# Turning and splitting queries and keys of two token tiles at a time, with the gate and pooling projections issued in even steps over the heads of a differential-attention encoder layer

## The chip, the cores and the metric

The kernel runs on one core of one Trainium2 chip. The metric is the device time of one execution in microseconds (us): lower is better. Three runs of the kernel before gave 1553.82, 1554.85 and 1556.53 us; their median is 1554.85 us.

## What is computed

One residual layer on 1024 tokens of 1024 channels, in float32. The part that the change touches is the projection of the normalised input h, and what attention makes of queries and keys:

```python
h = rmsnorm(x, g_mix[l])
z = h @ w_in[l]                                  # pooling channels | q | k | v
y_pool = pool_mixer(u_pool, w_pool_grp[l], pool_scale[l])
y_attn = diff_attention(q, k, v, ...)            # 8 heads, two softmax maps each, 64 channels a map
gates = sigmoid(h @ w_gate[l] + b_gate[l])
merged = gates[..., :D] * (y_pool @ w_branch_pool[l]) + gates[..., D:] * (y_attn @ w_branch_attn[l])
x = x + merged @ w_out[l]
x = x + square(relu(rmsnorm(x) @ w_up[l])) @ w_down[l]
```

The pooling mixer takes, for each of four groups of 128 channels, the mean over the last 2, 4, 8 or 16 tokens minus the token itself, and multiplies it by a 128x128 matrix.

## The kernel before

Every float32 operand of a matmul is split into a high part (rounded to the type that TensorE takes, by a cast on ScalarE) and a low part (the rest, by a subtraction on VectorE, or on GpSimd for weights). A product is then three matmuls into one PSUM bank: high x high, high x low, low x high. The helpers are `split` (L117 the cast, L118 the subtraction) and `mm3` (L123, L124, L125).

The work of the heads is a pipeline over 64 steps, one for each head h (8) and token tile t (8 tiles of 128 tokens). The loop over g at L645 runs one stage for each of several token tiles in every step, with the delays of the string `O`: A computes the projections z of a tile (24 matmuls of 384 columns), B normalises q and k and splits v (VectorE, ScalarE, GpSimd; the tile qn), C turns qn by transposes on TensorE into the bank tk and splits it into K and Q (`stage_qkT`, L453), D computes scores sc, their minimum (VectorE, L502) and the exponential (ScalarE, L510), E turns the attention weights s into the tiles AT (bank ta, L555, then split), F multiplies them by V (bank po), H and R the norm of the result (trr is a transpose of R), W loads and splits the next head's weights.

In stage C each map m of a tile takes three casts on ScalarE (L468, L470, L473) and three subtractions on VectorE (L469, L471, L472), on 64 partitions and 128 columns. The banks tk, ta and trr share two PSUM banks (`ps_t`).

Behind that loop in the code stand the gate and pooling projections, called units here: 16 column blocks of w_gate and four pooling groups, each for two halves of 512 tokens, so 40 units of 24 matmuls of 512 columns (g and u). A unit loads its weights by SP's queue (`fill_w`), splits them with ScalarE and GpSimd, multiplies, is emptied by ScalarE (`go`, L745, or L710 and L737) and stored by a DMA that ScalarE issues. A unit up to gate column 12, and all of the pooling group's, use the one bank of `ps_f`; the later columns alternate with the two banks of z. `pool_group` also makes running sums on VectorE (L719 to L728) and copies on GpSimd (L718).

The order of each engine is not the order of the code. A scheduler picks, for each engine, the next instruction among those that it holds to be ready, with the code's order as priority. The units at the end of the code are thus fetched forward into the heads. Behind the heads come the branch projections (bp, ba), the output projection (op), the feed-forward layer (X, Y, Z, W, then Da, Db).

Of the kernel before, what the change touches and what calls it, by code (L numbers as in the profile page):

```python
# [8 lines left out]
F32 = mybir.dt.float32  # L9
# [3 lines left out]
ALU = mybir.AluOpType  # L13
# [18 lines left out]

N_U, N_W, N_RAW, N_V = 11, 8, 2, 6
N_FW, N_FR, N_FO = 4, 2, 2
N_Q, N_QN = 3, 2
N_Z, N_S, N_T, N_F = 2, 2, 2, 1
N_YU = 5
N_QKVW = 8 * H
# [17 lines left out]
def encoder_kernel(  # L56
# [55 lines left out]
    def f(ap):  # L112
        return ap.bitcast(F32)
# [28 lines left out]
    def fr_tile(shape, name):  # L142
        return fp.tile(shape, F32, tag="fr", name=name, bufs=N_FR)
# [142 lines left out]
        }  # L286


    with ExitStack() as ph:
        sp = ph.enter_context(tc.tile_pool(name="sp", bufs=1))  # L290
        ps_s = ph.enter_context(tc.tile_pool(name="ps_s", bufs=N_S, space=PSUM))
# [161 lines left out]
        def stage_qkT(h, t):  # L453

            th, c0 = t // 4, (t % 4) * P
            K, qn = KV[h][0][th], st[h, t]["qn"]
            tr = ps_t.tile([P, 512], F32, tag="tr", name=f"tk{h}_{t}")
            for i in range(2):
                nc.tensor.transpose(
                    tr[:, i * P : (i + 1) * P], qn[:, 2 * i : 2 * i + 2, :].rearrange("p a b -> p (a b)"), identf  # L460
                )
            Q = sp.tile([P, 2, 2, P], F32R, tag="Q", name=f"Q{h}_{t}", bufs=N_Q)
            halves = (slice(0, HD), slice(HD, P))
            for m in range(2):
                own, other = halves[m], halves[1 - m]
                q, k = tr[own, 0:P], tr[own, P : 2 * P]
                k_hi, q_hi = K[own, m, c0 : c0 + P], Q[own, m, 0, :]
                nc.scalar.copy(k_hi, k)  # L468
                nc.vector.tensor_tensor(K[other, m, c0 : c0 + P], k, f(k_hi), op=ALU.subtract)  # L469
                nc.scalar.copy(q_hi, q)  # L470
                nc.vector.tensor_tensor(Q[other, m, 0, :], q, f(q_hi), op=ALU.subtract)  # L471
                nc.vector.tensor_tensor(Q[own, m, 1, :], q, f(q_hi), op=ALU.subtract)  # L472
                nc.scalar.copy(Q[other, m, 1, :], q)  # L473
            st[h, t]["Q"] = Q
            yield

        def stage_scores(h, t):
# [189 lines left out]
    def fill_w(src, c0, name):  # L667
        ws = []
        for j in range(2):
            rw = fr_tile([P, 4, P], f"fr{name}_{j}")  # L670
            nc.sync.dma_start(
                rw, src[j * 512 : (j + 1) * 512, c0 : c0 + P].rearrange("(kk p) c -> p kk c", p=P)
            )
            w = fw_tile([P, 2, 4, P], f"fw{name}_{j}")
            split(w[:, 0], w[:, 1], rw, nc.gpsimd)
            ws.append(w)
        return ws

    nb = [0]

    def spare_bank(name):

        nb[0] += 1
        pool, tag = (ps_f, "f") if nb[0] % 3 == 0 else (ps_z, "z")
        return pool.tile([P, 512], F32, tag=tag, name=name)

    def fill_bank(name):
        return ps_f.tile([P, 512], F32, tag="f", name=name)

    def fill_proj(ws, th, name, bank_fn=fill_bank):  # L690
        ps = bank_fn(name)
        for k in range(NK):
            w = ws[k // 4]
            mm3(
                ps, w[:, 0, k % 4, :], w[:, 1, k % 4, :],
                hT[k // 2, th, 0][:, k % 2, :], hT[k // 2, th, 1][:, k % 2, :], k == 0, k == NK - 1,
            )
        return ps

    def pool_group(g):  # L700
        win = WINDOWS[g]
        ws = fill_w(w_in, g * P, f"pool{g}")
        rg = fr_tile([P, P], f"rgrp{g}")
        nc.sync.dma_start(rg, w_pool_grp[g])
        wg = fq.tile([P, 2, P], F32R, tag="wg", name=f"wgrp{g}")
        split(wg[:, 0, :], wg[:, 1, :], rg, nc.gpsimd)
        u = fu_tile(f"u{g}")
        for th in range(2):
            ps = fill_proj(ws, th, f"u{g}_{th}")
            nc.scalar.copy(u[:, th * 512 : (th + 1) * 512], ps)  # L710

            n0 = 16 * th
            src = u[:, 512 * th - n0 : 512 * (th + 1)]
            n = 512 + n0
            cur, sh = src, 1
            while sh < win:
                nxt = fo_tile(f"sum{g}_{th}_{sh}")
                nc.gpsimd.tensor_copy(nxt[:, 0:sh], cur[:, 0:sh])  # L718
                nc.vector.tensor_tensor(nxt[:, sh:n], cur[:, sh:n], cur[:, 0 : n - sh], op=ALU.add)  # L719
                cur = nxt  # L720
                sh *= 2
            e = 0
            if th == 0:
                e = win - 1
                nc.vector.tensor_tensor(cur[:, 0:e], cur[:, 0:e], inv[:, 0:e], op=ALU.mult)
                nc.vector.tensor_tensor(cur[:, 0:e], cur[:, 0:e], src[:, 0:e], op=ALU.subtract)
            e += n0
            nc.vector.scalar_tensor_tensor(  # L728
                cur[:, e:n], cur[:, e:n], 1.0 / win, src[:, e:n], op0=ALU.mult, op1=ALU.subtract
            )  # L730
            m = fq.tile([P, 2, 512], F32R, tag="mx", name=f"mix{g}_{th}")
            split(m[:, 0, :], m[:, 1, :], cur[:, n0:n])
            yield
            ps = ps_f.tile([P, 512], F32, tag="f", name=f"yp{g}_{th}")
            mm3(ps, wg[:, 0, :], wg[:, 1, :], m[:, 0, :], m[:, 1, :], True, True)
            yp = fo_tile(f"yps{g}_{th}")
            nc.scalar.activation(yp[:, 0:512], ps, AF.Copy, scale=cols[:, 16 + g : 17 + g])  # L737
            nc.scalar.dma_start(p_dram[g * P : (g + 1) * P, th * 512 : (th + 1) * 512], yp[:, 0:512])

    def gate_cols(c):  # L740
        ws = fill_w(w_gate, c * P, f"gate{c}")
        for th in range(2):
            ps = fill_proj(ws, th, f"g{c}_{th}", spare_bank if c >= G_Z else fill_bank)
            fo = fo_tile(f"go{c}_{th}")
            nc.scalar.activation(fo[:, 0:512], ps, AF.Identity, bias=cols[:, c : c + 1])  # L745
            nc.scalar.dma_start(g_dram[c * P : (c + 1) * P, th * 512 : (th + 1) * 512], fo[:, 0:512])
            yield

    def gates():
        for c in range(2 * NK - 2):  # L750
            yield from gate_cols(c)
        for gen in [gate_cols(c) for c in (2 * NK - 2, 2 * NK - 1)] * 2:
            next(gen)
            yield
# [569 lines left out]
```

## Time and profile before

| what | value |
|---|---|
| median of three runs | 1554.85 us (1553.82 to 1556.53) |
| span of the profiled execution, first to last instruction | 1551.6 us |
| median of the runs less that span | 3.2 us |
| granted TensorE clock | 1.000 |
| instructions in the span | 22088 |
| heads (z, attention and the units) | about 10 to 700 us |

The profile is of one execution. The span is the time from its first to its last instruction; the runs' time has a little around it. PE is TensorE's matmuls, PEld its weight loads, DVE is VectorE, ACT ScalarE, POOL GpSimd, SP the queue that issues most DMAs. Busy times are shares of the span; "idle before" is the idle time of an engine ahead of an instruction, with the instruction that ended it.

### The profile page before, as it was taken

To read this page: it belongs to the slowest core of one execution; us is meant where nothing else is said; L and a number is where in the kernel's file an instruction comes from. 1 tells how busy PE (TensorE), PEld (TensorE's weight loads), DVE (VectorE), ACT (ScalarE), POOL (GpSimd) and SP (SyncE) were. 2 spreads that over 40 slices of the span, in tenths; PEclk is the share of its full clock that TensorE was granted. 3 is DMA by queue.
4 is the path that set the end of the run, shared out by engine and by line. 5 is a ranking of instruction groups with operands and counts; after the bars stand their busy time and mean duration, and the time that the engine had idled before them with its cause. 6 is when DMAs were issued, how large, how long until landed. Compare 5 with 4: busy or idle time off the path is not lost.

```text
span 1551.6 us, 22088 instructions
## 1 busy us (share of the span) xinstructions
PE 1533.6 (99%) x7649; PEld 1320.8 (85%) x7649; DVE 1011.3 (65%) x2277; ACT 816.7 (53%) x1810; POOL 354.8 (23%) x449
## 2 busy tenths in 40 slices
PE   7999999999999999999999999999999999999999
PEld 6999999999998989888888887888888788888887
DVE  7777677777878787746422458866665667556662
ACT  6656556656566555645532547565555633333331
POOL 5433334243525262324363400000000000000000
PEclk9999999999999999999999999999999999999999
DMA  7111212021202031248536534554343799437650
GB/s 229 51 53 48 66 41 68 24 75 37 75 28 83 28 96 42 69 147 284 179 122 210 168 112 124 182 185 155 129 142 109 278 334 370 170 122 257 224 190 27
DMA packets 168009, 206.94 MB, mean 133 GB/s; under 512 B 10117, under 2 KB 104026, under 8 KB 167898
## 3 DMA queue, kind: packets, MB, share of 16 engines
q1 hardware_dynamic: 150490, 178.23, 35.0%
q10 hardware_dynamic: 17408, 27.30, 4.7%
q8 instruction: 60, 0.98, 0.3%
q14 instruction: 51, 0.42, 0.1%
HBM read 150.94 MB, written 54.56 MB: 132 GB/s over the span
## 4 chain that ended last, share of the span: by engine, by line
PE 89%; DVE 4%; DMA 3%; ACT 1%; issue 1%; POOL 1%; SPq 0%; ACTq 0%; POOLq 0%; DVEq 0%
PE z L125 5%; PE z L123 5%; PE z L124 5%; PE Da L124 4%; PE Da L123 4%; PE Da L125 4%; PE g L123 3%; PE g L124 3%; PE g L125 3%; PE Db L124 3%; PE Db L123 3%; PE Db L125 3%; PE X L125 2%; PE X L123 2%; PE X L124 2%; PE sc L499 2%
## 5 line engine op out<-in xcount | busy, mean ns | idle before, releaser
L123 PE MATMUL z<-wqkv,hT 128*128 128x384 f32 x512 | 174.7, 342 | 0.4 <-DVE qn L441 0.3
L125 PE MATMUL z<-wqkv,hT 128*128 128x384 f32 x512 | 174.3, 341 | 0.5 <-DVE hT L118 0.5
L124 PE MATMUL z<-wqkv,hT 128*128 128x384 f32 x512 | 173.8, 339 | 0.0
L510 ACT ACTIVATE s<-s,nm 128x256 f32<-128x256 f32 (+7 forms) x128 | 99.6, 778 | 49.2 <-DVE nm L502 44.1
L249 POOL TENSOR_TENSOR ms<-ms,mhalf 128x4 f32<-128x4 f32 x64 | 66.6, 1040 | 157.7 <-DVE ms L248 139.1
L125 PE MATMUL g<-hT,fwgate 128*128 128x512 f32 x256 | 101.0, 394 | 0.0
L124 PE MATMUL g<-hT,fwgate 128*128 128x512 f32 x256 | 100.9, 394 | 0.0
L123 PE MATMUL g<-hT,fwgate 128*128 128x512 f32 x256 | 100.9, 395 | 0.0
L123 PEld LDWEIGHTS z<-wqkv,hT 128*128 128x128 f32 x512 | 96.9, 189 | 4.2 <-DVE qn L441 1.0
L125 PEld LDWEIGHTS z<-wqkv,hT 128*128 128x128 f32 x512 | 96.7, 189 | 3.3 <-DVE hT L118 1.3
L124 PEld LDWEIGHTS z<-wqkv,hT 128*128 128x128 f32 x512 | 96.8, 189 | 2.9
L502 DVE CUSTOM_DVE_ANT_0 s<-sc,dist 128x512 f32<-128x512 f32 (+3 forms) x128 | 74.7, 586 | 22.1 <-PE sc L500 20.7
L118 POOL TENSOR_TENSOR wqkv<-rqkv,wqkv 128x384 fp32r<-128x384 f32 x60 | 63.3, 1072 | 17.7 <-ACT wqkv L117 15.3
L499 PE MATMUL sc<-K,Q 128*128 128x512 f32 (+2 forms) x192 | 67.2, 355 | 0.1
L118 DVE TENSOR_TENSOR AS<-s,AS 128x512 fp32r<-128x512 f32 x64 | 43.8, 687 | 35.8 <-ACT AS L117 35.6
L500 PE MATMUL sc<-K,Q 128*128 128x512 f32 (+2 forms) x192 | 66.6, 354 | 0.0
L473 ACT CAST Q<-tk 64x128 fp32r<-64x128 f32 x128 | 33.2, 260 | 58.6 <-DVE Q L472 56.8
L447 POOL TENSOR_TENSOR qn<-qn,ggh 128x128 f32<-128x128 f32 x64 | 32.6, 510 | 137.5 <-DVE qn L441 124.2
L470 ACT CAST Q<-tk 64x128 fp32r<-64x128 f32 x128 | 33.1, 259 | 50.5 <-DVE K L469 49.1
L118 POOL TENSOR_TENSOR fwgate<-frgate,fwgate 128x512 fp32r<-128x512 f32 x32 | 45.2, 1416 | 52.2 <-ACT fwgate L117 52.0
L125 PEld LDWEIGHTS g<-hT,fwgate 128*128 128x128 f32 x256 | 48.1, 188 | 8.6
L123 PEld LDWEIGHTS g<-hT,fwgate 128*128 128x128 f32 x256 | 48.2, 188 | 7.1
(429 smaller groups left out, 4649.6 us busy)
## 6 DMA issues: line engine op xcount, KB each, us to landing
wd<-in_w_down_dram SPq DMA_DIRECT2D x56, 512.0 KB, 5.5
wu<-in_w_up_dram SPq DMA_DIRECT2D x32, 512.0 KB, 5.3
udS<-us SPq DMA_DIRECT2D x64, 256.0 KB, 2.5
ur<-udS SPq DMA_DIRECT2D x32, 512.0 KB, 3.2
rqkv<-in_w_in_dram SPq DMA_DIRECT2D x64, 192.0 KB, 2.8
ud<-u ACTq DMA_DIRECT2D x48, 256.0 KB, 2.2
ur<-ud SPq DMA_DIRECT2D x24, 512.0 KB, 5.5
frgate<-in_w_gate_dram SPq DMA_DIRECT2D x32, 256.0 KB, 2.6
```

The costliest lines, as they stand in the source:

```text
L118: return (lo_eng or nc.vector).tensor_tensor(lo, src, f(hi), op=ALU.subtract)
L123: nc.tensor.matmul(ps, lhs_hi, rhs_hi, start=first, stop=False, **kw)
L124: nc.tensor.matmul(ps, lhs_hi, rhs_lo, start=False, stop=False, **kw)
L125: nc.tensor.matmul(ps, lhs_lo, rhs_hi, start=False, stop=last, **kw)
L249: nc.gpsimd.tensor_tensor(dst, dst, mhalf[:, :n], op=ALU.pow)
L447: nc.gpsimd.tensor_tensor(qn[:, 2:4, :], qn[:, 2:4, :], ggh.unsqueeze(1).broadcast_to([P, 2, HD]), op=ALU.mult)
L470: nc.scalar.copy(q_hi, q)
L473: nc.scalar.copy(Q[other, m, 1, :], q)
L499: nc.tensor.matmul(dst, Q[:, i, 0, :], rhs, start=True, stop=False)
L500: nc.tensor.matmul(dst, Q[:, i, 1, :], rhs, start=False, stop=True)
L502: nc.vector.tensor_tensor_reduce(out=s[i][:, c : c + w], in0=sc[:, 0:w], in1=dist[:, o0 + c : o0 + c + w], scale=2.0 ** -(h + 1), scalar=B ...
L510: nc.scalar.activation(s[i][:, 0:n], s[i][:, 0:n], AF.Exp, bias=last, scale=-1.0, accum_out=Z[:, i, t : t + 1])
```

## The change

Stage C runs once for two token tiles, at the odd one: four transposes fill the whole bank tk (queries of both tiles in the first half, keys in the second), and each of the twelve casts and subtractions covers 256 columns. Buffers: two tiles Q of twice the width instead of three, three qn instead of two. All stages behind C start one step later. The units' functions move ahead of the heads' loop, and the loop issues them itself: from step 5 on, half a unit for each step, 34 in all; six are left for the end. With that, their place in the code's order, and so their priority, is among the heads.

```diff
-N_Q, N_QN = 3, 2
+N_Q, N_QN = 2, 3
...
-O = "B1 C2 H6 D3 R7 E4 F5 W-2 A0"
+O = "B1 C2 H7 D4 R8 E5 F6 W-2 A0"
 ORDER = [(w[0], int(w[1:])) for w in O.split()]
 G_FIRST, G_Z = 13, 13
+F_FROM, F_PACE, F_UNITS = 4, 0.5, 34
...
+    def fillers():
+        gate_units = gates()
+        for _ in range(G_FIRST):
+            next(gate_units)
+            yield
+        for g in range(4):
+            for _ in pool_group(g):
+                yield
+                next(gate_units)
+                yield
+        for _ in gate_units:
+            yield
...
         def stage_qkT(h, t):
 
             th, c0 = t // 4, (t % 4) * P
-            K, qn = KV[h][0][th], st[h, t]["qn"]
+            K = KV[h][0][th]
             tr = ps_t.tile([P, 512], F32, tag="tr", name=f"tk{h}_{t}")
-            for i in range(2):
-                nc.tensor.transpose(
-                    tr[:, i * P : (i + 1) * P], qn[:, 2 * i : 2 * i + 2, :].rearrange("p a b -> p (a b)"), identf
-                )
-            Q = sp.tile([P, 2, 2, P], F32R, tag="Q", name=f"Q{h}_{t}", bufs=N_Q)
+            tk = tr.rearrange("p (s t q) -> p s t q", s=2, t=2)
+            for j in range(2):
+                qn = st[h, t + j]["qn"]
+                for i in range(2):
+                    nc.tensor.transpose(
+                        tk[:, i, j, :], qn[:, 2 * i : 2 * i + 2, :].rearrange("p a b -> p (a b)"), identf
+                    )
+            Q = sp.tile([P, 2, 2, 2 * P], F32R, tag="Q", name=f"Q{h}_{t}", bufs=N_Q)
             halves = (slice(0, HD), slice(HD, P))
+            c1 = c0 + 2 * P
             for m in range(2):
                 own, other = halves[m], halves[1 - m]
-                q, k = tr[own, 0:P], tr[own, P : 2 * P]
-                k_hi, q_hi = K[own, m, c0 : c0 + P], Q[own, m, 0, :]
+                q, k = tr[own, 0 : 2 * P], tr[own, 2 * P : 4 * P]
+                k_hi, q_hi = K[own, m, c0:c1], Q[own, m, 0, :]
                 nc.scalar.copy(k_hi, k)
-                nc.vector.tensor_tensor(K[other, m, c0 : c0 + P], k, f(k_hi), op=ALU.subtract)
+                nc.vector.tensor_tensor(K[other, m, c0:c1], k, f(k_hi), op=ALU.subtract)
                 nc.scalar.copy(q_hi, q)
                 nc.vector.tensor_tensor(Q[other, m, 0, :], q, f(q_hi), op=ALU.subtract)
                 nc.vector.tensor_tensor(Q[own, m, 1, :], q, f(q_hi), op=ALU.subtract)
                 nc.scalar.copy(Q[other, m, 1, :], q)
-            st[h, t]["Q"] = Q
+            for j in range(2):
+                st[h, t + j]["Q"] = Q[:, :, :, j * P : (j + 1) * P]
             yield
...
-            elif w == "C":
-                yield from stage_qkT(h, t)
+            elif w == "C" and t % 2:
+                yield from stage_qkT(h, t - 1)
...
-        for g in range(-2, N + 8):
+        units, made = fillers(), 0
+        for g in range(-2, N + 10):
...
+            while made < F_UNITS and made < (g - F_FROM) * F_PACE:
+                next(units)
+                made += 1
+        for _ in units:
+            pass
...
-    gate_units = gates()
-    for _ in range(G_FIRST):
-        next(gate_units)
-    for g in range(4):
-        for _ in pool_group(g):
-            next(gate_units)
-    for _ in gate_units:
-        pass
```

What the scheduler makes of it is shown at three places. Names are the program's, with head and tile behind the letter (AT0_3_4l is of head 0 and the fourth pair of tiles); "ISA" on VectorE is the fused add with minimum (L502) or the sum of squares (L593).

The first is on VectorE, at the end of head 0, ahead of the subtraction into AT0_3_4l that frees a transposed bank. Before:

```order
L517 RECIPROCAL cf0_7_1286<-Z0_361 128x1
L518 SCALAR_TENSOR_TENSOR cf0_7_1286<-cf0_7_1286,Z0_361,nlam_233 128x1
L437 TENSOR_REDUCE ms1_4_1532<-sq1_4_1531 128x4
L593 ISA oq0_2_1309,SS0_362<-po0_2_1261,identf_90 128x128
L593 ISA SS0_362 128x1
L519 SCALAR_TENSOR_TENSOR s0_7_0_1241<-s0_7_1_1242,cf0_7_1286,s0_7_0_1241 128x1024
L593 ISA oq0_2_1309,SS0_362<-po0_2_1261,identf_90 128x128
L593 ISA SS0_362 128x1
L248 TENSOR_SCALAR ms1_4_1532<-ms1_4_1532 128x4
L118 TENSOR_TENSOR AT0_3_4l_1251<-ta0_6_1_1290,AT0_3_4h_1250 128x3x128
```

After, at the same subtraction:

```order
L627 RECIPROCAL cf0_7_1372<-Z0_361 128x1
L628 SCALAR_TENSOR_TENSOR cf0_7_1372<-cf0_7_1372,Z0_361,nlam_233 128x1
L119 TENSOR_TENSOR AT0_3_4l_1337<-ta0_6_1_1376,AT0_3_4h_1336 128x3x128
L629 SCALAR_TENSOR_TENSOR s0_7_0_1327<-s0_7_1_1328,cf0_7_1372,s0_7_0_1327 128x1024
L703 ISA oq0_2_1395,SS0_362<-po0_2_1347,identf_90 128x128
```

The subtraction into AT0_3_4l stood behind the product over s0_7 of 1024 columns (L519) and two sums; now it stands ahead of them (L629 is that product).

The second is on VectorE, in head 6, at the first subtraction into AT6_1_0l and the running sums of pooling group 3 (sum3_0). Before:

```order
L719 TENSOR_TENSOR sum3_0_4_8118<-sum3_0_2_8115 128x508
L719 TENSOR_TENSOR sum3_0_8_8121<-sum3_0_4_8118 128x504
L728 SCALAR_TENSOR_TENSOR sum3_0_8_8121<-sum3_0_8_8121,u3_8085 128x497
L725 TENSOR_TENSOR sum3_0_8_8121<-sum3_0_8_8121,inv_99 128x15
L502 ISA s6_4_1_5977,nm6_4_5978<-sc6_4_1_0_5999,dist_229 128x512
L502 ISA nm6_4_5978 128x1
L726 TENSOR_TENSOR sum3_0_8_8121<-sum3_0_8_8121,u3_8085 128x15
L118 TENSOR_TENSOR AT6_1_0l_5851<-ta6_2_0_5854,AT6_1_0h_5850 128x3x128
L502 ISA s6_4_1_5977,nm6_4_5978<-sc6_4_1_512_6003,dist_229,nm6_4_5978 128x128
```

After:

```order
L612 ISA s6_4_0_6638,nm6_4_6640<-sc6_4_0_512_6664,dist_229,nm6_4_6640 128x128
L612 ISA nm6_4_6640 128x1
L119 TENSOR_TENSOR AT6_1_0l_6498<-ta6_2_0_6501,AT6_1_0h_6497 128x3x128
L546 TENSOR_TENSOR qn6_7_6631<-z6_7_6522,ms6_7_6624 128x256
L342 TENSOR_TENSOR sum3_0_1_6605<-u3_6578 128x511
L612 ISA s6_4_1_6639,nm6_4_6640<-sc6_4_1_0_6669,dist_229 128x512
L612 ISA nm6_4_6640 128x1
L119 TENSOR_TENSOR AT6_1_0l_6498<-ta6_3_0_6645,AT6_1_0h_6497 128x4x128
L342 TENSOR_TENSOR sum3_0_2_6608<-sum3_0_1_6605 128x510
L612 ISA s6_4_1_6639,nm6_4_6640<-sc6_4_1_512_6673,dist_229,nm6_4_6640 128x128
```

All the sums of group 3 now come behind the subtraction out of ta6_2_0 (the first, of 511 columns, right behind the next qn), and the long ones behind the subtraction out of ta6_3_0 as well.

The third is on TensorE near the end of the heads, between the units g11_0 and g11_1, that share the one bank of `ps_f`. Before:

```order
L125 MATMUL g11_0_8290<-hT3_0_0_147,fwgate11_1_8287 128x512
L499 MATMUL sc7_4_1_512_6806<-K7_1_6089,Q7_4_6656 128x256
L459 MATMUL tk7_5_6759<-identf_90,qn7_5_6650 128x128 x2
L500 MATMUL sc7_4_1_0_6802<-K7_0_6088,Q7_4_6656 128x512
L500 MATMUL sc7_4_1_512_6806<-K7_1_6089,Q7_4_6656 128x256
L555 MATMUL ta7_3_0_6786<-identf_90,s7_3_6669 128x128 x4
L123 MATMUL g11_1_8318<-hT0_1_0_321,fwgate11_0_8282 128x512
```

After (the transposes ta7_4_0 and two matmuls of po7_1 stand just ahead):

```order
L126 MATMUL g11_0_7657<-hT3_0_0_147,fwgate11_1_7654 128x512
L124 MATMUL g11_0_7657<-hT3_0_0_147,fwgate11_1_7654 128x512
L125 MATMUL g11_0_7657<-hT3_0_1_148,fwgate11_1_7654 128x512
L126 MATMUL g11_0_7657<-hT3_0_0_147,fwgate11_1_7654 128x512
L609 MATMUL sc7_5_1_0_7616<-K7_0_6654,Q7_4_7393 128x512
L610 MATMUL sc7_5_1_0_7616<-K7_0_6654,Q7_4_7393 128x512
L609 MATMUL sc7_5_1_512_7620<-K7_1_6655,Q7_4_7393 128x256
L610 MATMUL sc7_5_1_512_7620<-K7_1_6655,Q7_4_7393 128x256
L665 MATMUL ta7_4_1_7629<-identf_90,s7_4_0_7535 128x128
L609 MATMUL sc7_6_0_0_7692<-K7_0_6654,Q7_6_7572 128x512
L610 MATMUL sc7_6_0_0_7692<-K7_0_6654,Q7_6_7572 128x512
L124 MATMUL g11_1_7798<-hT0_1_0_321,fwgate11_0_7649 128x512
```

And on ScalarE after the change, from the cast that ta7_4_0 releases to the one that empties g11_0:

```order
L118 CAST AT7_2_0h_7592<-ta7_4_0_7597 128x4x128
L620 ACTIVATE s7_5_0_7585,Z7_6658<-s7_5_0_7585,nm7_5_7587 128x768
L689 ACTIVATE oq7_1_7640<-po7_1_7604 128x256
L690 COPY oS7_1_7639<-po7_1_7604 128x256
L368 ACTIVATE go11_0_7682<-g11_0_7657,cols_116 128x512
```

Between the last matmul of g11_0 and the first of g11_1 there stand other rows than before; on ScalarE an exponential of 768 columns and two copies of po7_1 stand ahead of go11_0.

More of the change, by code (lines that the diff above doesn't have):

```diff
@@ L286, in alloc_T, with fill_w, spare_bank @@
         }
+    def fill_w(src, c0, name):
+        ws = []
+        for j in range(2):
+            rw = fr_tile([P, 4, P], f"fr{name}_{j}")
+            nc.sync.dma_start(
+                rw, src[j * 512 : (j + 1) * 512, c0 : c0 + P].rearrange("(kk p) c -> p kk c", p=P)
+            )
+            w = fw_tile([P, 2, 4, P], f"fw{name}_{j}")
+            split(w[:, 0], w[:, 1], rw, nc.gpsimd)
+            ws.append(w)
+        return ws
+    nb = [0]
+    def spare_bank(name):
+        nb[0] += 1
+        pool, tag = (ps_f, "f") if nb[0] % 3 == 0 else (ps_z, "z")
+        return pool.tile([P, 512], F32, tag=tag, name=name)
@@ new lines, in gate_cols, with gates @@
+    def gate_cols(c):
+        ws = fill_w(w_gate, c * P, f"gate{c}")
+        for th in range(2):
+            ps = fill_proj(ws, th, f"g{c}_{th}", spare_bank if c >= G_Z else fill_bank)
+            fo = fo_tile(f"go{c}_{th}")
+            nc.scalar.activation(fo[:, 0:512], ps, AF.Identity, bias=cols[:, c : c + 1])
+            nc.scalar.dma_start(g_dram[c * P : (c + 1) * P, th * 512 : (th + 1) * 512], fo[:, 0:512])
+            yield
+    def gates():
+        for c in range(2 * NK - 2):
+            yield from gate_cols(c)
+        for gen in [gate_cols(c) for c in (2 * NK - 2, 2 * NK - 1)] * 2:
+            next(gen)
+            yield
@@ L289, in encoder_kernel @@
+    def fillers():
[5 more added lines that the diff above has]
+            for _ in pool_group(g):
+                yield
+                next(gate_units)
+                yield
+        for _ in gate_units:
+            yield
     with ExitStack() as ph:
@@ L473, in stage_qkT @@
                 nc.scalar.copy(Q[other, m, 1, :], q)
-            st[h, t]["Q"] = Q
+            for j in range(2):
+                st[h, t + j]["Q"] = Q[:, :, :, j * P : (j + 1) * P]
             yield
@@ L664, in encoder_kernel @@
                     pass
[L667 to L754, printed above, removed]
```

49 lines of the change are left out of this document (added).

## The prediction

> **What bounds the kernel now.** I read the page's line of engines first.
>
> ```profile
> PE 1533.6 (99%) x7649; PEld 1320.8 (85%) x7649; DVE 1011.3 (65%) x2277; ACT 816.7 (53%) x1810; POOL 354.8 (23%) x449
> ```
>
> TensorE is busy for 99% of the span. That number is modelled, so it needs a second reading: busy time by stretches of 25 us. The columns are PE, PEld, DVE, ACT, POOL, clock, DMA share and GB/s.
>
> ```profile
> 0.00:25.00 25.00, 15.63 (x76) 13.77 (x77) 15.85 (x38) 15.34 (x35) 12.91 (x40) 1.00 0.92 275
> 25.00:50.00 25.00, 24.82 (x148) 22.47 (x147) 20.01 (x54) 15.56 (x44) 12.64 (x13) 1.00 0.28 92
> 100.00:125.00 25.00, 24.36 (x145) 22.34 (x144) 17.86 (x56) 12.89 (x35) 4.30 (x7) 1.00 0.05 17
> 475.00:500.00 25.00, 24.70 (x141) 22.33 (x140) 20.51 (x63) 15.14 (x42) 10.96 (x16) 1.00 0.24 77
> 550.00:575.00 25.00, 23.96 (x129) 20.66 (x128) 21.61 (x59) 14.63 (x40) 14.80 (x18) 1.00 0.30 98
> 725.00:750.00 25.00, 25.00 (x111) 20.60 (x110) 14.50 (x19) 19.49 (x32) 12.32 (x8) 1.00 0.72 227
> ```
>
> The last row holds only matmuls of 512 columns: 25 us / 111 = 0.225 us each, at clock 1.00. The heads fill 25 to 700 us, and every stretch of theirs that isn't shown reads 25.00. So TensorE lacks 0.18 + 0.64 + 0.30 + 1.04 = **2.16 us** in all the heads. The first row's gap is the start, whose first 78 matmuls stand in the same order after the change. The view of waits, TensorE's rows over the whole span, names who made it wait.
>
> ```profile
> PE hps L275 <- DVE hn L270: 8.8, 1, 8.8
> PE X L123 <- ACT U L1075: 2.0, 2, 1.3
> PE ta L555 <- DVE AT_0l L118: 1.0, 1, 1.0
> PE ta L555 <- DVE AT_4l L118: 0.6, 1, 0.6
> PE z L123 <- DVE qn L441: 0.3, 1, 0.3
> ```
>
> Three waits on VectorE in the heads (1.0, 0.6, 0.3) are nearly all that a change to the heads can take away. VectorE and ScalarE have time to spare; what they do counts only where one instruction comes late. Two places in the timeline show why one did.
>
> ```profile
> 475.14 1.30 POOL L118 TENSOR_TENSOR fwgate<-frgate,fwgate 128x512 fp32r<-128x512 f32 x1
> 475.33 1.13 DVE L725 TENSOR_TENSOR sum<-sum,inv 128x7 f32<-128x7 f32 x1
> 478.77 0.42 DVE L441 TENSOR_TENSOR qn<-z,ms 128x256 f32<-128x256 f32 x1
> 479.24 0.45 PE L123 MATMUL z<-wqkv,hT 128*128 128x384 f32 x1 [0.30 <-DVE qn L441]
> ...
> 556.00 1.71 POOL L118 TENSOR_TENSOR fwgate<-frgate,fwgate 128x512 fp32r<-128x512 f32 x1 [0.19 <-ACT fwgate L117]
> 556.58 1.65 DVE L728 SCALAR_TENSOR_TENSOR sum<-sum,u 128x497 f32<-128x497 f32 x1
> 558.32 0.18 DVE L725 TENSOR_TENSOR sum<-sum,inv 128x15 f32<-128x15 f32 x1
> 559.11 0.55 DVE L118 TENSOR_TENSOR AT_0l<-ta,AT_0h 128x384 fp32r<-128x384 f32 x1
> 559.80 0.63 PE L555 MATMUL ta<-identf,s 128*128 128x128 f32 x4 [0.95 <-DVE AT_0l L118]
> ```
>
> At 475.33 a VectorE instruction of 7 columns took 1.13 us, where one of 15 columns took 0.18 at 558.32. It ended at 476.46, with the GpSimd instruction that had begun before it (475.14 + 1.30 = 476.44). That cost VectorE 0.95 us. The 1.65 us at 556.58 outlasted its GpSimd neighbour too (556.00 + 1.71 = 557.71). TensorE waited 2 to 3 us later for what stood behind in VectorE's queue. So two of the waits come from the pooling mixer's sums on VectorE falling beside weight splits on GpSimd.
>
> **The change part by part.** *Turning and splitting pairs.* The pieces of one token tile:
>
> ```profile
> L469 DVE TENSOR_TENSOR K<-tk,K 64x128 fp32r<-64x128 f32 x128 | 37.0, 289 | 16.3 <-ACT K L468 12.4
> L471 DVE TENSOR_TENSOR Q<-tk,Q 64x128 fp32r<-64x128 f32 x128 | 37.0, 289 | 20.2 <-ACT Q L470 17.1
> L470 ACT CAST Q<-tk 64x128 fp32r<-64x128 f32 x128 | 33.1, 259 | 50.5 <-DVE K L469 49.1
> L118 DVE TENSOR_TENSOR AT<-ta,AT 128x256 fp32r<-128x256 f32 x16 | 6.7, 418 | 0.2
> L117 ACT CAST AT<-ta 128x256 fp32r<-128x256 f32 x16 | 5.9, 369 | 3.7 <-PE ta L555 3.7
> ```
>
> No 64x256 operation is in the trace. Two of 128 columns bound it above (2 x 289 and 2 x 259), one below; I take the split of an attention tile of 256 columns, also out of PSUM: 418 and 369 ns. VectorE: 384 x 0.289 = 111.0 us become 192 x 0.418 = 80.3, so 30.7 us less. ScalarE: 384 x 0.259 = 99.5 become 192 x 0.369 = 70.8, so 28.7 less. All of it lies beside a TensorE that is busy, and is worth nothing by itself. If 64x256 took twice 64x128, it would save nothing and cost nothing. TensorE's own share is unchanged: 7649 matmuls of the same forms, transposes in fours instead of twos. I cost that at 0.
>
> *Even steps.* They move instructions, and add none. The projections ran between the heads already, since the scheduler had fetched them forward. The stretch rows of the gate matmuls alone (PE, PEld, ACT):
>
> ```profile
> 25.00:50.00 25.00, 8.47 (x31) 5.56 (x32) 0.69 (x1) 1.00 0.28 92
> 650.00:675.00 25.00, 19.08 (x77) 13.63 (x76) 2.06 (x3) 1.00 0.26 80
> ```
>
> So nothing is won by overlap; only which instruction stands ahead of which changes. At the wait of 559.80 it helps: in VectorE's order the split into AT6_1_0l that TensorE waited for now stands ahead of the sums. At 479.24 qn5_7 stands ahead of the sums of group 2. At the third, in the stretch 100 to 125, the split into AT0_3_4l stands ahead of the long product over s0_7. I clear all three: 0.64 + 0.30 + 1.04 = **-1.98 us**, bounds -2.16 and 0. The DMAs that move with the units (weights on SP's queue, stores on ScalarE's) I cost at 0: in the three stretches the DMA share is 0.05, 0.24 and 0.30.
>
> *A new wait at the end.* Up to gate column 12 each unit needs the one PSUM bank of ps_f, which ScalarE empties. Behind g11_0 the rows of the order leave TensorE this much until g11_1 from the end of the transposes ta7_4_0: four matmuls of 256 columns, eight of 512, one transpose. The pace of 256 columns is 0.12 (starts of two neighbours):
>
> ```profile
> 662.59 0.28 PE L125 MATMUL po<-AT_0h,V 128*128 128x256 f32 x1
> 662.71 0.28 PE L123 MATMUL po<-AT_0h,V 128*128 128x256 f32 x1
> ```
>
> That is 4 x 0.12 + 8 x 0.225 + about 0.13 (four transposes at 559.80 end after 0.63) = 2.41 us. ScalarE's queue holds, between the cast that these transposes release and go11_0:
>
> ```profile
> L117 ACT CAST AT_0h<-ta 128x512 fp32r<-128x512 f32 x40 | 23.4, 584 | 5.6 <-PE ta L555 4.9
> L510 ACT ACTIVATE s<-s,nm 128x768 f32<-128x768 f32 x16 | 15.0, 939 | 4.5 <-DVE nm L502 4.2
> L510 ACT ACTIVATION_READ_ACCUMULATOR s<-s,nm 128x1 f32 x128 | 24.1, 188 | 0.0
> L579 ACT ACTIVATE oq<-po 128x256 f32<-128x256 f32 x32 | 12.3, 383 | 10.0 <-PE po L125 9.9
> L580 ACT COPY oS<-po 128x256 f32<-128x256 f32 x32 | 11.8, 368 | 0.0
> L745 ACT ACTIVATE go<-g,cols 128x512 f32<-128x512 f32 x32 | 21.9, 686 | 12.6 <-PE g L125 10.6 <-issue 1.9
> ```
>
> 584 + 939 + 188 + 383 + 368 + 686 = 3.15 us, so TensorE waits **+0.74 us**; behind it stand all later matmuls. Bounds: 0 (the exponential comes early) and 2 x 0.74 (yp3_1 to g10_1 has 1.25 us, also close).
>
> Sum: 1551.6 - 1.98 + 0.74 = 1550.4 us of span. The median of the runs, 1554.85, lies 3.2 us above the span (what comes ahead of the first and behind the last instruction); kept, that makes **1553.6 us**.
>
> **The rivals.** *The waits move, and don't go.* GpSimd's splits and the mixer's sums are as many as before, and a hit costs VectorE about 0.95 us. The Trainium skill, "SBUF — State Buffer", section "SBUF: two separate sides", says that a VectorE instruction with two SBUF inputs and a GpSimd instruction exclude each other for a whole instruction. The two rows at 475 and 556 agree; by that rule alone I would clear none of the three waits. Here it would mean two or three waits of 0.3 to 1.0 us at new places: 1554.85 - 1.98 + 0.74 + 2 = 1555.6. Against it: VectorE has 30.7 us less to do in 675 us, so a late instruction catches up sooner. The case that the scheduler had already spread the projections, and the change does nothing, ends here too.
>
> *The pair comes late (slower).* ScalarE and VectorE take turns on the bank of a transposed tile. From the last transpose to the last cast:
>
> ```profile
> 131.69 0.38 PE L459 MATMUL tk<-identf,qn 128*128 128x128 f32 x2
> 136.57 0.26 ACT L473 CAST Q<-tk 64x128 fp32r<-64x128 f32 x1 [0.16 <-DVE Q L472]
> ...
> 382.84 0.38 PE L459 MATMUL tk<-identf,qn 128*128 128x128 f32 x2
> 393.11 0.26 ACT L473 CAST Q<-tk 64x128 fp32r<-64x128 f32 x1 [0.35 <-DVE Q L472]
> ```
>
> 4.8 us at best, 10.1 at worst. A pair adds 6 x 0.129 + 6 x 0.110 = 1.4 us. Summed along the order, TensorE's first use of the last cast follows 7.5 us or more behind the transposes before, and 8.7 or more after; seven of the 32 pairs have under 10 us, five of them a head's third and fourth tile. If their chains lie near the worst (10.1 + 1.4), each waits up to 2.8 us, and 1 us at a chain of some 10: 7 us, so 1553.6 + 7 = 1560.6; the point from which it decides is a chain of 8.7 us. Against it: the same engines have less queued, and median distance grew from 9.3 to 12.4 us.
>
> *More idle time than the rows show (faster).* The two waits X <- ACT U in the feed-forward stage (2.0 us) could go as well, if ScalarE gets there with less behind it: 1554.85 - 2.16 - 2.0 = 1550.7, with no new wait. Against it: TensorE's order from bp0_1 on is the same row for row. The Trainium skill, "Perfetto Trace Analysis", section "Identifying the Most-Contended Engine", calls matmul busy time a bad measure and wants the weight-load share. That share, 22.3 to 22.5 of 25 in three of these stretches against 20.6 where the pace is 0.225, shows no hidden room in the heads.
>
> **How the numbers follow.** Forecast 0.45 (1552.6 to 1554.8), waits move 0.18 (1554.3 to 1556.5), pair late 0.17 (1556.5 and up), more idle time 0.20 (1552 and down). A measurement tells about 0.2%, 3.1 us, from no change: under 1551.7 is faster, over 1558.0 slower. Nearly all of the fourth and most of the third case pass these bounds: faster 0.19, within 0.66, slower 0.15. The range, 1550.6 to 1558.0, takes in the bounds of both unknown terms and leaves out the tails of the last two cases.
>
> **What would show it.** Right: the splits of queries and keys near 0.42 and 0.37 us; the stretches of 100, 475 and 550 us at 25.00; a wait of g on the go of ScalarE near 638 us. Wrong: waits of sc or ta on the last cast of Q (pair late); new waits ahead of which a sum took over 1 us (waits move); the waits on U gone (more idle time). If 64x256 took 0.58 us, the relief of VectorE falls, and with it the first step.

## The result and the profile after

The changed kernel takes **1551.66 us** (median of 20 runs, 1550.49 to 1554.12), the kernel before 1554.59 us (20 runs, 1553.82 to 1556.53). The ratio is 0.9981, 95% interval 0.9975 to 0.9988: 2.9 us less. The interval leaves out 1, so the gain is clear of the scatter, though it is just inside the 0.2% that the prediction calls no change. The prediction's 1553.6 us was 1.9 us too high; the range held the time.

The profiled execution after has a span of 1551.5 us, as long as that of before (1551.6). Both are untypical: the spans of the 20 runs have a median of 1549.9, and the profiled one lost some 1.7 us to a clock drop in the feed-forward stage, shown below; 38 runs of the kernel before, taken later, have spans around 1552.5, 0.9 us above the profiled one. So the two profiles are compared stretch by stretch, not by their spans.

Engines, from the page of the changed kernel:

```profile
PE 1533.1 (99%) x7649; PEld 1322.8 (85%) x7649; DVE 982.9 (63%) x2085; ACT 792.3 (51%) x1618; POOL 354.0 (23%) x449
```

VectorE has 28.4 us less to do than before, ScalarE 24.4. The pieces of a pair, from the groups by shape:

```profile
L578 DVE TENSOR_TENSOR K<-tk,K 64x256 fp32r<-64x256 f32 x64 | 27.0, 422 | 14.3 <-ACT K L577 12.7
L579 ACT CAST Q<-tk 64x256 fp32r<-64x256 f32 x64 | 23.6, 368 | 23.6 <-DVE K L578 22.5
```

422 and 368 ns stand against the 418 and 369 that were taken from the 128x256 rows. The stretches that the prediction watches, and two more (columns as there):

```profile
25.00:50.00 25.00, 23.77 (x144) 21.94 (x144) 21.04 (x50) 14.00 (x40) 11.09 (x14) 1.00 0.29 90
100.00:125.00 25.00, 25.00 (x151) 23.21 (x150) 17.69 (x54) 14.10 (x35) 6.50 (x10) 1.00 0.12 37
475.00:500.00 25.00, 25.00 (x146) 23.34 (x145) 17.66 (x56) 12.85 (x31) 7.93 (x9) 1.00 0.12 37
550.00:575.00 25.00, 25.00 (x146) 23.32 (x145) 19.35 (x57) 12.66 (x32) 10.13 (x15) 1.00 0.18 59
625.00:650.00 25.00, 24.55 (x128) 20.68 (x127) 14.93 (x44) 13.28 (x32) 6.03 (x9) 1.00 0.22 72
1225.00:1250.00 25.00, 23.16 (x95) 18.55 (x94) 17.64 (x21) 13.52 (x19) 0.00 (x0) 0.93 0.71 247
```

The three gaps at 100, 475 and 550 us are closed. A gap of 1.23 us stands at 25, one of 0.45 at 625. TensorE's waits name them:

```profile
PE hps L276 <- DVE hn L271: 8.9, 1, 8.9
PE X L124 <- ACT U L1092: 2.5, 2, 1.8
PE hps L276 <- DVE hT L119: 1.2, 1, 1.2
...
PE sc L609 <- DVE nm L612: 0.4, 1, 0.4
```

Gaps are not all. I took for each matmul the distance to the start of the next, less the pace of its form (229 ns at 512 columns, 174 at 384, 118 at 256, 108 at 128), and summed it by stretch of the span, in us:

```
kernel                   span  0-50  50-500  500-700  700-940  940-1200  1200-1260
before                 1551.6   5.7     4.3      2.5      1.4       1.7        1.4
before, again          1553.5   7.3     4.2      2.5      0.9       2.0        1.6
changed                1551.5   6.9     2.3      1.3      1.0       1.6        3.6
pairs alone            1567.3   5.6     5.4     17.7      0.5       1.8        1.5
units alone            1556.2   7.7     4.2      2.5      1.3       1.7        4.0
pairs in halves        1553.4   7.7     2.4      1.7      0.9       1.7        4.1
18 units in the loop   1558.4   7.3     2.5      8.7      0.7       2.5        1.4
delay alone            1554.4   6.5     5.1      3.3      1.7       1.8        1.6
first unit one later   1549.1   5.1     2.8      1.2      1.0       1.5        2.5
from 8, pace 0.6       1557.3   5.3     3.0      0.9      9.2       2.3        1.7
delay and units        1561.9   7.2     7.4      2.5      6.5       1.8        1.3
from 6, pace 0.51      1549.5   6.0     2.8      1.4      1.0       1.5        1.8
from 6, pace 0.52      1547.8   5.1     2.5      0.8      1.4       1.8        1.0
```

Between 50 and 700 us the loss fell from 6.8 to 3.6 us. That is the gain. Of these 3.2 us, 2.0 are distances over 0.2 us too long (2.6 us before, 0.6 after: the waits); 1.2 lie in smaller ones, whose cause I did not isolate.

### The profile page after: what moved, and what is told of

Same layout as the page of the kernel before. It is cut to its first block, busy times and chain, and to the rows that moved or that the text cites. A ratio compares the mean times of both kernels' runs of the same rounds, so it can differ in the third digit from the quotient of the medians.

```text
span 1551.5 us, 21682 instructions
## 1 busy us (share of the span) xinstructions
PE 1533.1 (99%) x7649; PEld 1322.8 (85%) x7649; DVE 982.9 (63%) x2085; ACT 792.3 (51%) x1618; POOL 354.0 (23%) x449
## 4 chain that ended last, share of the span: by engine, by line
PE 94%; DMA 2%; DVE 2%; ACT 1%; SPq 1%; issue 0%; DVEq 0%; ACTq 0%
PE z L126 6%; PE z L124 6%; PE z L125 6%; PE Da L125 4%; PE g L126 4%; PE Da L124 4%; PE g L125 4%; PE g L124 4%; PE Da L126 4%; PE Db L125 3%; PE Db L124 3%; PE Db L126 3%; PE X L126 2%; PE X L124 2%; PE X L125 2%; PE sc L609 2%
## 5 line engine op out<-in xcount | busy, mean ns | idle before, releaser
L119 POOL TENSOR_TENSOR wqkv<-rqkv,wqkv 128x384 fp32r<-128x384 f32 x60 | 63.3, 1070 | 14.8 <-ACT wqkv L118 12.9
L126 PEld LDWEIGHTS g<-hT,fwgate 128*128 128x128 f32 x256 | 48.1, 188 | 9.6
L124 PEld LDWEIGHTS g<-hT,fwgate 128*128 128x128 f32 x256 | 48.1, 188 | 9.1 <-ACT go L368 0.2
L125 PEld LDWEIGHTS g<-hT,fwgate 128*128 128x128 f32 x256 | 48.1, 188 | 8.8
L126 PE MATMUL ba<-yT,wba 128*128 128x512 f32 x128 | 50.6, 395 | 0.0
L124 PE MATMUL ba<-yT,wba 128*128 128x512 f32 x128 | 50.6, 395 | 0.0
```

The lines of the kernel that those rows point to most:

```text
L119: return (lo_eng or nc.vector).tensor_tensor(lo, src, f(hi), op=ALU.subtract)
L124: nc.tensor.matmul(ps, lhs_hi, rhs_hi, start=first, stop=False, **kw)
L125: nc.tensor.matmul(ps, lhs_hi, rhs_lo, start=False, stop=False, **kw)
L126: nc.tensor.matmul(ps, lhs_lo, rhs_hi, start=False, stop=last, **kw)
```

## The experiments

The theory after the result, **A**: the gain is the three waits, cleared by another order of the instructions; the engine time that the pairs save is worth nothing. Rivals: **B**, that saved time lets late instructions catch up; **C**, that the even steps bring the gain.

**The kernel before, again.** No edit.

> The kernel before, unchanged, to see how its executions scatter and what lies between span and time. The changed kernel's runs have their time 1.8 us above their span. If that holds here, the runs have spans of about 1552.8 (1554.6 less 1.8), and the profiled span of 1551.6 on which the prediction rests was a quick execution by about 1.2 us. If the 3.2 us of the prediction are real, the spans are about 1551.4.

1554.36 us (11 runs), ratio 0.9998 (0.9989 to 1.0007). Time less span is 1.8 us in each of its runs, and in those of the kernel before beside them (27, median span 1552.5). The 3.2 us of the prediction were not a constant. This execution also shows a wait that the first one lacked:

```profile
PE hps L275 <- DVE hT L118: 0.7, 1, 0.7
PE ta L555 <- DVE AT_4l L118: 0.6, 1, 0.6
```

So a wait at the start belongs to the kernel before too, in one of its two profiled executions; the three waits in the heads are here again, within 0.1 us.

**Pairs alone.**

```diff
-F_FROM, F_PACE, F_UNITS = 4, 0.5, 34
+F_FROM, F_PACE, F_UNITS = 4, 0.5, 0
```

> Pairs of token tiles as in the change, but no unit issued in the loop: all 40 units stand behind the heads in the code, as before. Theory A (the order of the instructions, and the extra step between the stages, clear the three waits; the engine time saved is worth nothing): the subtraction into AT0_3_4l, qn5_7 and the subtraction into AT6_1_0l stand ahead of the long products here too, so no waits there, and the weight splits of the first unit fall later than in the changed kernel, so its wait of 1.2 us at 28.7 us is not there: 1550.5 to 1552. Theory C (the even steps bring the gain): 1554.6, as before, with the three waits.

**1569.05 us**, 0.95% slower than before (ratio 1.0095, 1.0081 to 1.0109). Neither theory foresaw it. TensorE's waits:

```profile
PE u L124 <- ACT yps L360: 3.4, 3, 1.8
PE yp L124 <- ACT go L368: 2.2, 3, 0.8
...
PE g L124 <- ACT go L368: 1.9, 3, 0.8
PE g L124 <- ACT u L333: 1.2, 2, 0.7
...
PE g L124 <- ACT yps L360: 0.8, 1, 0.8
```

3.4 + 2.2 + 1.9 + 1.2 + 0.8 = 9.5 us, all between units and ScalarE's emptying of the bank of `ps_f`. The gate matmuls by stretch (PE busy and count), here and in the changed kernel:

```profile
600.00:650.00 50.00, 18.08 (x74) 1.00 0.30 91
650.00:700.00 50.00, 45.54 (x190) 0.97 0.27 89
700.00:750.00 50.00, 17.34 (x77) 1.00 0.88 286
```

```profile
600.00:650.00 50.00, 26.20 (x108) 1.00 0.22 74
650.00:700.00 50.00, 42.38 (x180) 1.00 0.44 142
700.00:750.00 50.00, 0.00 (x0) 1.00 0.81 255
```

With the pairs, the scheduler left to itself fetches the units forward later: in TensorE's order 393 unit matmuls stand behind the last transposes of the attention weights, against 82 before and 123 in the changed kernel. The last three gate columns (144 matmuls) have three banks; what is late beyond them waits for one. The clock of 0.97 in 650 to 700 adds 1.5 us. Lateness isn't all of it: between 50 and 500 us too, ahead of all these waits, the pairs alone lose 5.4 us, and the changed kernel 2.3. The three waits of before are gone from their places, but others have come (sc on nm at 216 us, 0.8 us; two of ta on VectorE, 0.3 and 0.2 us).

**Units alone.** The changed kernel with stage C, the delays and the buffers of before:

```diff
-N_Q, N_QN = 2, 3
+N_Q, N_QN = 3, 2
...
-O = "B1 C2 H7 D4 R8 E5 F6 W-2 A0"
+O = "B1 C2 H6 D3 R7 E4 F5 W-2 A0"
...
-            elif w == "C" and t % 2:
-                yield from stage_qkT(h, t - 1)
+            elif w == "C":
+                yield from stage_qkT(h, t)
```

> Units issued in the loop as in the change, but queries and keys turned and split one token tile at a time, with the stages' delays and buffers of before. Theory A: the order of VectorE's instructions is that of before row for row and TensorE's differs in six rows at the start, so the three waits of 1.0, 0.6 and 0.3 us stand, and the wait of 1.2 us at the start may come in addition: 1554.6 to 1556. Theory C (even steps bring the gain): 1551.7.

1556.80 us, ratio 1.0014 (1.0005 to 1.0023), 0.8 us over what A allowed: C falls. VectorE's order is that of before row for row, the other engines' differ in a few rows at the start; so the waits are those of before, with a longer one at the start:

```profile
PE hps L276 <- DVE hT L119: 1.4, 1, 1.4
PE ta L660 <- DVE AT_0l L119: 0.9, 1, 0.9
PE ta L660 <- DVE AT_4l L119: 0.6, 1, 0.6
...
PE z L124 <- DVE qn L546: 0.3, 1, 0.3
```

Between 50 and 700 us it loses 6.7 us, as the repeated kernel before does. What it costs lies, in this execution, behind the wait on U (4.0 us against 1.6) and a little at the start (7.7 against 7.3).

Alone, the parts cost 14.7 and 2.5 us; together they gain 2.9. The even steps gain nothing by themselves: they hold the units where the scheduler had put them without pairs.

**Pairs in halves.** In the changed kernel each of the twelve operations of a pair becomes two, as here for the first two:

```diff
-                nc.scalar.copy(k_hi, k)
-                nc.vector.tensor_tensor(K[other, m, c0:c1], k, f(k_hi), op=ALU.subtract)
+                for s in ab:
+                    nc.scalar.copy(k_hi[:, s], k[:, s])
+                for s in ab:
+                    nc.vector.tensor_tensor(k_lo[:, s], k[:, s], f(k_hi[:, s]), op=ALU.subtract)
```

> The changed kernel, but each of the twelve casts and subtractions of a pair is cut into two of 64x128, so that VectorE and ScalarE do as much work as before (1011 and 817 us busy), with two tiles a step and the changed delays kept. Theory A: within 1 us of the changed kernel, 1551 to 1552.7. Theory B (the 28 us of VectorE and 24 us of ScalarE that the wider operations save are what lets late instructions catch up): back to about 1554.6, with new waits on VectorE in the heads.

1552.35 us, ratio 0.9986 (0.9977 to 0.9995), so most of the gain stays, and the three waits stay away. B is not borne out. The test is weaker than meant:

```profile
L588 DVE TENSOR_TENSOR Q<-tk,Q 64x128 fp32r<-64x128 f32 x128 | 31.6, 284 | 0.9
```

128 pieces of 284 ns fill only 31.6 us of busy time, not 36.4, since each pair of pieces overlaps in part. VectorE came to 997.7 us and ScalarE to 801.4, so 14.8 of the 28.4 us saved on the one and 9.1 of the 24.4 on the other were put back. Between 50 and 700 us this run loses 4.1 us, the changed kernel 3.6. So all of the saved time may be worth some 1 us there, an estimate from one execution of each; the interval of the times doesn't exclude more.

**18 units in the loop.**

```diff
-F_FROM, F_PACE, F_UNITS = 4, 0.5, 34
+F_FROM, F_PACE, F_UNITS = 4, 0.5, 18
```

> The changed kernel, but only 18 of the 40 units are issued in the loop. In TensorE's order 216 unit matmuls then stand behind the last transposes of the attention weights, against 123 in the changed kernel and 393 with the pairs alone (1569.05 us). Theory D (the units that pairs leave late must pass one PSUM bank that ScalarE empties, 0.9 us of waiting for each): 144 matmuls, the last three gate columns, have three banks, so 72 go through the one bank, and some more ahead of them: three to eight waits of 0.9 us, 1554 to 1560, waits of g, u and yp on yps, go and u of ScalarE. Theory E (pairs alone are slow for what they do to VectorE and ScalarE in the heads): the time stays near 1569 whatever the number of units in the loop, or the waits are on other names.

1559.50 us, ratio 1.0036 (1.0023 to 1.0048), as theory D has it: 123, 216 and 393 late matmuls give 1.3, 8.7 and 17.7 us of loss in 500 to 700 us. Its waits are g and u and yp on ScalarE again (1.3 + 1.1 + 0.5 us), and one of trr on GpSimd's r (1.4 us); together these are 4.3 of the 7.4 us more than in the changed kernel.

**The delay alone.** The kernel before with these lines, and the loop two steps longer:

```diff
-N_Q, N_QN = 3, 2
+N_Q, N_QN = 4, 2
...
-O = "B1 C2 H6 D3 R7 E4 F5 W-2 A0"
+O = "B1 C2 H7 D4 R8 E5 F6 W-2 A0"
```

> The kernel before with the delays of the changed kernel (every stage behind the turning of queries and keys one step later, four tiles Q), without pairs and without units in the loop. Theory A1 (the extra step is the slack that clears the three waits): the waits at 122, 479 and 560 us are gone and the time is 1552 to 1553.5. Theory A2 (any other order would clear them as well, and set up others): one or two are gone, others come, 1553.5 to 1555.5. If the pairs themselves are needed: 1554.4 or more with the three waits in place.

1556.38 us, ratio 1.0014 (1.0005 to 1.0023). The two waits of ta are gone. A wait of z on qn stands at another place (547 us), and others have come:

```profile
PE sc L499 <- DVE nm L502: 0.6, 3, 0.3
PE bp L123 <- ACT go L745: 0.5, 1, 0.5
PE z L123 <- DVE qn L441: 0.5, 1, 0.5
PE g L123 <- ACT go L745: 0.4, 1, 0.4
```

A2, and a little worse. An extra step of slack clears a wait, and the order that comes with it sets up others.

**Delay and units, without the pair** (the kernel of units alone, with the two lines above).

> Delays of the changed kernel and units issued in the loop, but token tiles turned and split one at a time (four tiles Q). Everything of the change except the pair. If delay and units together make the gain and the pair adds only engine time that TensorE never waits for: 1551 to 1553. If the pair's larger pieces (four transposes and twelve wide operations every second step) are needed for an order without waits: 1554.4 or more, as with the delay alone (1556.4) and the units alone (1556.8). The first unit's weight splits fall beside hn as in the changed kernel, so a wait of 1.2 to 1.4 us at the start is expected in both cases.

1560.99 us, ratio 1.0047 (1.0034 to 1.0059). So the pair is part of the gain. Of the 8.4 us by which its span exceeds that of the repeated kernel before, 5.6 lie behind the heads (700 to 940 us: 6.5 against 0.9), where bp waited 2.9 us for ScalarE's rT, with 53 late unit matmuls to cover it. But in the heads too (50 to 700 us) it lost 9.9 us, against 6.7 there and 3.6 in the changed kernel; z waited 0.9 us for qn, yp and g 0.6 and 0.5 for go.

The table's column from 50 to 500 us sorts all the kernels. The seven that have both pairs and units in the loop lose 2.3 to 3.0 us there, the six that lack one of the two 4.2 to 7.4. So the gain in the heads needs both, and it isn't one lucky order; with half of the saved engine time put back it stays (2.4).

**The first unit one step later.**

```diff
-F_FROM, F_PACE, F_UNITS = 4, 0.5, 34
+F_FROM, F_PACE, F_UNITS = 5, 0.5, 34
```

> The changed kernel with its first unit one step later. On GpSimd both weight splits of the first unit then stand behind the fill of the distances, as before, and not one ahead of it. If such splits beside the four products hn on VectorE cost them about 1 us each (2.94 and 3.01 us with none beside them, 3.97 with one, 4.81 to 5.00 with two), hn takes 2.9 to 4.0 us here and the wait of hps on hT falls from 1.2 to between 0 and 0.7 us: 1550.4 to 1551.3, unless the other order of the heads sets up a new wait. If the splits have nothing to do with it, the wait stays at 1.2 us: 1551.7.

**1550.81 us**, ratio 0.9976 (0.9967 to 0.9985). The wait at the start is gone. The four products hn on VectorE and the first unit's weight splits on GpSimd, in the changed kernel, in the kernel before again, and here:

```profile
23.44 4.81 DVE L271 SCALAR_TENSOR_TENSOR hn<-x,rs,gmb 128x512 f32<-128x512 f32 x4
23.82 1.52 POOL L119 TENSOR_TENSOR fwgate<-frgate,fwgate 128x512 fp32r<-128x512 f32 x1 [0.23 <-ACT fwgate L118]
25.57 1.47 POOL L119 TENSOR_TENSOR fwgate<-frgate,fwgate 128x512 fp32r<-128x512 f32 x1
28.73 0.63 PE L276 MATMUL hps<-identf,hn 128*128 128x128 f32 x4 [1.23 <-DVE hT L119]
```

```profile
24.28 3.97 DVE L270 SCALAR_TENSOR_TENSOR hn<-x,rs,gmb 128x512 f32<-128x512 f32 x4
26.17 3.22 POOL L118 TENSOR_TENSOR fwgate<-frgate,fwgate 128x512 fp32r<-128x512 f32 x2 [0.74 <-ACT fwgate L117]
```

```profile
23.33 2.93 DVE L271 SCALAR_TENSOR_TENSOR hn<-x,rs,gmb 128x512 f32<-128x512 f32 x4
26.58 2.54 POOL L119 TENSOR_TENSOR fwgate<-frgate,fwgate 128x512 fp32r<-128x512 f32 x2 [2.10 <-ACT fwgate L118]
```

Both splits within the products' time: 4.81 us. The first split within it (the products end at 28.25): 3.97. None (they end at 26.26): 2.93. A split costs the products it falls beside about 1 us. In the changed kernel the first split stands ahead of a fill on GpSimd, here behind it, and that row moves it clear of the products. It does not decide alone: the kernel before has the same order in both of its executions, and its products took 2.94 us in the first and 3.97 in the second, in which they started 1.3 us later.

**The end of the heads.** Three more settings of the pace.

```diff
-F_FROM, F_PACE, F_UNITS = 4, 0.5, 34
+F_FROM, F_PACE, F_UNITS = 8, 0.6, 34
```

> The changed kernel with the first unit four steps later and six tenths of a unit in each step, so that only 3 unit matmuls are left behind the last transposes of the attention weights, against 123. By the reading that units late mean waits for the one bank, no units late is best: no wait at 638 us, 1550 to 1551. By the rival, that TensorE needs some 20 us of units to fill the time in which the last head's chain (minimum, exponential, transposes, split, sums, norm) goes through VectorE and ScalarE: waits of 1 to 3 us each of sc, ta, po and bp in 650 to 710 us, 1555 to 1565.

1558.98 us, ratio 1.0027 (1.0018 to 1.0036): the rival is right, though in one wait on another name than those listed:

```profile
PE trr L721 <- POOL r L719: 4.7, 1, 4.7
```

With 3 late unit matmuls nothing covers the last head's norm. Between that and the one bank lies the best supply:

```diff
-F_FROM, F_PACE, F_UNITS = 4, 0.5, 34
+F_FROM, F_PACE, F_UNITS = 6, 0.51, 34
```

> The changed kernel with its first unit two steps later and 0.51 of a unit in each step; 123 unit matmuls are left behind the last transposes of the attention weights, as in the changed kernel. If what counts is that no split falls beside hn and that some 120 are left, as in the kernel with the first unit one step later (1550.81): 1550.3 to 1551.3. If the exact order decides as much: a new wait of 0.3 to 1 us somewhere, up to 1552.5.

1550.58 us, ratio 0.9977 (0.9968 to 0.9986). One more step of supply:

```diff
-F_FROM, F_PACE, F_UNITS = 4, 0.5, 34
+F_FROM, F_PACE, F_UNITS = 6, 0.52, 34
```

> The same with 0.52 of a unit in each step: 86 unit matmuls are left behind the last transposes, near the 82 of the kernel before. If the fill at the end of the heads runs short only well below that (3 left cost some 5 us of waiting for trr), 1550.3 to 1551.5. If it runs short here already: a wait of trr on r of some 1 us or more, 1552 or more.

**1550.10 us**, ratio 0.9974 (0.9964 to 0.9984), the lowest of all and 0.2 us under the expected range. With 86 late matmuls TensorE's only waits in the heads are two of 0.3 us, of z on hT at the start. The three settings with a later first unit and 86 to 123 late matmuls all lie under the changed kernel, by 0.6 to 1.1 us if the ratios are compared (each group of runs has its own runs of the kernel before); the interval of each alone overlaps with its interval.

## Why the prediction was right and wrong

**The three waits: size right, cause wrong.** 1.98 us of gaps were to go, and went. But the step that failed is the one headed "Even steps": it gave them the moves that clear the waits. The run with units alone has VectorE's order unchanged and the waits in place. With the pairs alone the three waits are gone from their places, and with the delay alone the two of ta, but other waits come; the orders without them are those with pairs and units in the loop. I had compared two whole orders and put the difference down to the part of the diff that spoke of order. The even steps' other work, to keep the units from coming late, I did not see at all; without them the change costs 14.7 us.

**The pairs: right.** 80.3 and 70.8 us were expected for the pieces; 192 x 0.422 = 81.0 and 192 x 0.368 = 70.7 were measured. The engines' whole busy time fell a little less than expected (28.4 against 30.7 us, 24.4 against 28.7). That this is worth nothing by itself is borne out only in part, to within the 1 us or so that the halves leave. No wait of sc or ta on the last cast of Q came.

**The new wait at the end: place right, name wrong.** No wait of g on go, but one of 0.45 us at 638 us:

```profile
637.54 0.69 DVE L612 CUSTOM_DVE_ANT_0 s<-sc,dist 128x512 f32<-128x512 f32 x1 [0.17 <-PE sc L610]
637.99 0.71 ACT L368 ACTIVATE go<-g,cols 128x512 f32<-128x512 f32 x1
638.29 0.50 PE L609 MATMUL sc<-K,Q 128*128 128x512 f32 x1 [0.45 <-DVE nm L612]
638.86 0.39 PE L124 MATMUL g<-hT,fwgate 128*128 128x512 f32 x1
```

The scores waited for a minimum on VectorE; meanwhile go11_0 got done (637.99 + 0.71 = 638.70), 0.16 us ahead of g11_1. Without the first wait TensorE would have stood at g11_1 some 0.3 us too early (an estimate: 638.86 - 0.45 = 638.41, against 638.70): two waits at one place count once.

**The size: under half of the gain.** Forecast were 1.24 us less than before, measured 2.9. (The rest of the error of 1.9 us is the base: 1554.85 from three runs, 1554.59 from twenty.) The 3.2 us on top of the span are not this miss. They aren't the time around the span, which is 1.8 us in each run; but span and distance add up to the median of before, whatever the span was. With 1.8 us in their place the sum would give 1552.2, nearer by luck, since the quick execution that was profiled would have hidden part of the missing gain.

What was too small is the step that lets TensorE lack only 2.16 us in the heads. It counts idle time. As distances from start to start the three waits come to 2.4 us, some 0.16 more each than their idle time, and 1.2 us went in distances under 0.2 us, which the prediction put at nothing: it read no hidden room from the weight loads. What closed them stays open. The other way, the new wait of 0.74 us came to 0.6 by the same measure.

**The rivals.** "The waits move" came true once, at the start: 1.23 us behind hn, by splits beside VectorE. Sums in the heads were still hit (the longest of them took 1.80 us against a median of 0.70), but behind none did TensorE wait. The Trainium skill, "SBUF — State Buffer", section "SBUF: two separate sides", gives the rule that a VectorE instruction with two SBUF inputs and a GpSimd instruction that reads SBUF hold each other off, the later one waiting for the whole of the earlier. The steps from 2.93 to 3.97 and 4.81 us agree with it. "The pair comes late" did not happen. The time of 1551.66 us lies in the band of "More idle time" (1552 and down, 0.20), not in the forecast's own. But that came about in another form: the waits on U stayed (2.5 us), and 1.2 us went in distances too small for the view of waits.

## What to carry over

Before you credit one part of a change with the moves of a scheduler, compare the orders of the parts alone; parts that lose singly can gain together. Filler work has a best supply: too much left to the end runs into its own bank, too little leaves the last chain bare. Forecast the difference: a base that is a median of runs needs no time around the span. And idle time is not all that a busy engine loses; sum the distances between its starts as well.

## What was not expected of the hardware

**The clock after a wait.** In the changed kernel's feed-forward stage TensorE waited 1.84 us for U until 1232.75. What followed shows in the clock records. In all 13 traces every change of the granted clock lies a whole number of windows of 3.413 us behind the first record (in the changed kernel 357, 358 and 450). Cut into such windows:

```profile
1230.27:1233.69 3.42, 1.58 (x7) 1.00 (x6) 3.42 (x4) 2.78 (x5) 0.00 (x0) 1.00 1.07 383
1233.69:1237.10 3.41, 3.41 (x10) 2.62 (x9) 2.95 (x4) 2.33 (x3) 0.00 (x0) 0.50 0.92 363
1237.10:1240.51 3.41, 3.41 (x16) 2.76 (x16) 2.19 (x4) 2.31 (x4) 0.00 (x0) 1.00 0.02 7
```

The window of the wait had 1.84 us of idle TensorE (3.42 - 1.58), and the next one ran at 0.50: 3.41 x 0.50 = 1.7 us of clock lost. After the 4.7 us wait for r, in the kernel from 8 at pace 0.6, the clock stayed at 0.50 for two windows:

```profile
715.32:718.74 3.42, 0.00 (x0) 0.00 (x0) 2.32 (x3) 1.24 (x3) 2.76 (x3) 1.00 0.98 358
718.74:722.15 3.41, 2.69 (x7) 1.91 (x8) 0.26 (x1) 2.18 (x3) 1.55 (x2) 0.50 0.53 186
722.15:725.57 3.42, 3.42 (x10) 2.65 (x9) 0.69 (x1) 1.74 (x4) 0.00 (x0) 0.50 0.45 141
```

Yet after a wait of 2.30 us, in the kernel with its first unit one step later, it stayed at 1.00. There the end of a window cut the wait in two, of 0.7 and 1.6 us:

```profile
1227.02:1230.43 3.41, 2.69 (x12) 1.88 (x10) 3.38 (x6) 2.95 (x3) 0.00 (x0) 1.00 0.79 276
1230.43:1233.85 3.42, 1.84 (x8) 1.54 (x9) 2.46 (x3) 2.48 (x4) 0.00 (x0) 1.00 1.05 397
1233.85:1237.26 3.41, 3.41 (x17) 2.83 (x16) 3.41 (x4) 1.92 (x3) 0.00 (x0) 1.00 0.73 293
```

In the 13 traces 11 whole windows at 1.00 have 1.84 us or more of idle TensorE (six of them at the end of the program), and behind each the clock was 0.50. Of the windows at 1.00 with 1.75 us or less only one was followed by 0.50 (1.61 us, from two waits, with the pairs alone). So in these traces it is the idle time within one window that counts, from about half of it on, and where the windows fall is chance.

The Trainium skill, "TensorE: Matmul & The Clock Gate", section "Part 1: The HAM clock gate", says that the clock halves after an idle window of about 3.4 us that runs freely. The length agrees; but here a window that was idle for 1.84 of its 3.41 us was enough, and the measurement decides. A wait of 1.84 us thus cost 3.5: of the changed kernel's 20 runs, the two that list a mean clock of 0.999 instead of 1.000 have the two longest spans (1551.5 and 1552.3 us).
